# Experts in groups of 32 slots on four 32-column tiles of the array, results added back in quarter rows

## The chip, the cores and the metric

The kernel runs on one core of a Trainium2 chip. The metric is device time in microseconds of one execution. The engines of the core work side by side, each through its own program in order: TensorE (PE) multiplies and transposes, VectorE (DVE) and ScalarE (ACT) work element by element and empty PSUM, GpSimd (POOL) issues the indirect transfers and some element work, and SyncE (SP) issues nearly all other transfers. The 16 DMA engines of the core move what all queues ask for.

## The reference

One layer of a diffusion backbone over 512 latent tokens and 256 context tokens of width 1024, in 32-bit floats: modulated RMSNorm, one input projection, a gated short convolution beside grouped-query attention, an output projection with a gated residual, and then a mixture of experts, which takes most of the time:

```
logits = h @ w_router + b_router                 # 512 tokens x 32 experts
top_logit, top_idx = top_k(logits, 4); gate = softmax(top_logit)
for every expert e, over the tokens that chose it:
    gu = x @ w_gate_up[e] + b_gate_up[e]         # 1024 -> 2048
    y  = clamped_swiglu(gu) @ w_down[e] + b_down[e]   # 1024 -> 1024
    out[token] += gate * y
x = x + gt2 * out; return rmsnorm(x, g_final)
```

Each of the 32 experts has 8.39 MB of gate and up weights and 4.19 MB of down weights; they are read once. 2048 pairs of token and expert are spread over the experts. With the inputs used, the reference's router gives the largest expert 97 tokens, the next four 96, 94, 89 and 88, and the 17th by size 62.

## The kernel before

The first part (to about 330 us) computes norms, projections, attention, convolution and the router. Then the experts follow in an order of turns i = 0 to 31, sorted on chip by token count: `sort` ranks the experts, `place(i)` says which rank is worked on in turn i. Even turns are "heavy" (the 16 largest, 128 slots), odd turns are "light" (the other 16, 64 slots). What an expert has beyond its slots goes to a loop in `overflow`, which runs only if its block count is above zero. All engines meet at that branch, once.

Weights come in chunks of 1 MB, 128 partitions x 8 KB: 8 gate-up chunks `gu` (one for each 128 rows of the contraction) and 4 down chunks `dn` per turn. The list `seq` gives their order: of turn i first three gate-up chunks, then the four down chunks of turn i-1, then the other five gate-up chunks. `fetch` (L107 to L128) issues the next chunk of this list on SP's queue each time that a chunk has been used up; each fetch waits for PE to release the buffer that it refills, and for one of eight completion semaphores used in turn. There are 18 such buffers once all pools are open.

A heavy turn multiplies a chunk in four matmuls, 128 slots stationary and 512 weight columns moving, with the full array (L1017 gate-up, L1048 down). A light turn holds only 64 slots: two matmuls with 64 stationary columns each lie beside each other in the array, one for the low and one for the high half of the weight columns, so that slots 0 to 63 of PSUM hold one half of the output and partitions 64 to 127 the other (L1019, L1050). Each 32-bit matmul is two records in the trace. A bias matmul closes the gate-up sums (L1028, L1030).

Around them, per turn: `gather(i)` (L1200) reads the tokens' rows from the normed activations H2 by an indirect transfer on POOL's queue, `turn_x(i)` (L1212) transposes them, `activate` (L1224 to L1227) computes the clamped SwiGLU, `turn_a` (L1246) transposes its result, `put_back` weighs the down result by the gate (L1259, L1271) and `scatter` (L1253) adds it to ACC in HBM by an indirect accumulating transfer on POOL's queue. Each scatter waits for the one before it to land, since both add to ACC; POOL is in order, so what stands behind a waiting scatter waits too. Heavy and light turns have gather buffers of their own (`xgH`, `xgL`). The last turn's result is not scattered but multiplied back to the token rows on PE; ACC is read back (`sum` chunks) after the scatter of turn 30, added, normed and written out.

Of the kernel before, what the change touches and what calls it, by code (L numbers as in the profile page):

```python
# [35 lines left out]
P = 128  # L36
D = 1024
# [19 lines left out]
FULL = E // 2  # L57
CAP = 64
# [14 lines left out]
def dit_block(ctx, tc, x, c, cx, c_ctx, w_ada, b_ada, g_norm1, g_norm2, w_in, g_q, g_k, w_conv, w_out,  # L73
# [98 lines left out]
    nm2 = cst.tile([P, 1], F32)  # L172
# [86 lines left out]
    def place(i):  # L259

        return i // 2 if i % 2 == 0 else FULL + i // 2

# [36 lines left out]
    def places():  # L299
# [6 lines left out]
        half = float(SEQ + 1 + CAP)  # L306
# [4 lines left out]
        V.scalar_tensor_tensor(pm513, col[:, 0:1], -float(CAP), p513, op0=OP.mult, op1=OP.add)  # L311
        V.tensor_scalar(nm2, col[:, 0:1], -2.0, None, op0=OP.add)
        V.tensor_scalar(sgn, pm513, float(SEQ + 1 + E), -1.0, op0=OP.is_ge, op1=OP.mult)
# [639 lines left out]
    gt2l = m1.tile([P, 512], F32, name="gt2l")  # L953
    for _ in range(RING2):
        fetch()
    for q in range(4):
        DQ.dma_start(braw[q * E:(q + 1) * E, :].rearrange("e (m n) -> e m n", m=2),
                     raw_ap(b_gate_up, (q // 2) * 512, [[F2, E], [D, 2], [1, 512]]))
# [48 lines left out]

    def first_products(i, k):
        w, q = chunks.pop(("gu", i, k)), place(i)
        if k == 0:  # L1010
            gu[i] = [pair("S"), pair("R")] if heavy(i) else pair("J")
# [10 lines left out]
        if k < KC - 1:  # L1022
            return
        for m in range(2):
            b_ = bias[:, m * 512:(m + 1) * 512]
            if heavy(i):
                for n in range(2):
                    T.matmul(a[m][:, n, :], sel[:, n, q:q + 1].to_broadcast([P, P]), b_, start=False, stop=True)  # L1028
            else:
                T.matmul(a[:, m, :], sel2[i], b_, start=False, stop=True)  # L1030

    sel2 = {}

    def spread_sel(i):
        sel2[i] = m1.tile([P, 2 * CAP], F32R, name="sel2")
        V.tensor_copy(sel2[i].rearrange("p (n c) -> p n c", n=2),  # L1036
                      sel[:, :, place(i):place(i) + 1].to_broadcast([P, 2, CAP]))

    def second_products(i, j):
        w = chunks.pop(("dn", i, j))  # L1040
        if j == 0:
            dn[i] = pair("R") if heavy(i) else bank("V")
        for r in range(2):
            for n in range(2):
                c_ = slice(r * D + n * 512, r * D + (n + 1) * 512)
                start, stop = j == 0 and r == 0, j == 3 and r == 1
                if heavy(i):
                    T.matmul(dn[i][:, n, :], aT[i][:, 2 * j + r, :], w[:, c_], start=start, stop=stop)  # L1048
                else:
                    T.matmul(dn[i][n * CAP:(n + 1) * CAP, :], aT[i][:, j % 2 * 2 + r, j // 2 * CAP:(j // 2 + 1) * CAP],  # L1050
                             w[:, c_], start=start, stop=stop)
        fetch()

    sel = m1.tile([P, 2, E], F32R, name="sel")
    perm = m1.tile([2 * E, 2, E], F32, name="perm")
# [4 lines left out]
    at = cst.tile([2 * E, 1], F32)  # L1060

# [33 lines left out]

    tabs2 = cst.tile([P, 4, FULL], F32)
    idx = cst.tile([P, 2, FULL], I32)

    def slot_tables():

        p_ = bank("T")
        pv = perm.rearrange("p a e -> p (a e)")
        T.matmul(p_[:, 0:2 * E], tabA, pv, start=True, stop=True)
        for n in range(2):
            T.matmul(p_[n * CAP:(n + 1) * CAP, 2 * E:4 * E], tabA[:, 0:CAP], pv, start=True, stop=True)
        for h in range(2):
            V.tensor_copy(tabs2[:, h:4:2, :], p_[:, 2 * E * h:2 * E * h + 2 * E].rearrange(
                "p (a e) -> p a e", a=2)[:, :, FULL * h:FULL * h + FULL])
        ad_ = m1.tile([P, 2, FULL], F32, name="ad")
        V.tensor_scalar(ad_[:, 0, :], tabs2[:, 0, :], 0.0, p513, op0=OP.is_equal, op1=OP.mult)  # L1110
        V.tensor_scalar(ad_[:, 1, :], tabs2[:, 1, :], 0.0, pm513, op0=OP.is_equal, op1=OP.mult)
        V.scalar_tensor_tensor(idx[:, 0, :], tabs2[:, 0, :], -1.0, ad_[:, 0, :], op0=OP.add, op1=OP.add)
        V.tensor_add(ad_[:, 1, :], tabs2[:, 1, :], ad_[:, 1, :])
        V.tensor_scalar(idx[:, 1, :], ad_[:, 1, :], 2.0, nm2, op0=OP.mult, op1=OP.add)
        V.tensor_scalar(tabs2[:, 2:4, :], tabs2[:, 2:4, :], 1.0 / ALPHA, None, op0=OP.mult)

    def column(i):

        q = place(i) % FULL
        return idx[:, i % 2, q:q + 1], tabs2[:, 2 + i % 2, q:q + 1], tabs2[:, i % 2, q:q + 1]  # L1120


    def biases():
# [3 lines left out]
        V.tensor_scalar(braw[:, 512:D], braw[:, 512:D], 1.0, None, op0=OP.add)  # L1127
# [31 lines left out]
    def count_blocks(part):  # L1159

        if part == 0:
            nb = state["nb"] = m1.tile([E, NT + 2], F32, name="nb")
            V.tensor_scalar(nb[:, 0:1], at[0:E, :], float(FULL), float(P - CAP), op0=OP.is_ge, op1=OP.mult)
            V.tensor_add(nb[:, 0:1], nb[:, 0:1], cnt[0:E, :])
# [31 lines left out]
    H2h, ACCh = (x_.rearrange("r (n d) -> (r n) d", n=2) for x_ in (H2, ACC))  # L1196

    def gather(i):
        t = m2.tile([P, D if heavy(i) else 512], F32, name="xgH" if heavy(i) else "xgL")
        G.indirect_dma_start(out=t, out_offset=None, in_=H2[:, :] if heavy(i) else H2h,  # L1200
                             in_offset=bass.IndirectOffsetOnAxis(ap=column(i)[0], axis=0))
        xg[i] = t

    def turn_x(i):
        n = KC if heavy(i) else 4
        xT[i] = xp.tile([P, n, P], F32, name="xT", tag="xh" if heavy(i) else "xl")
        t = xg.pop(i)
        for hf in range(n // 4):
            p_ = bank("TV"[hf])
            for k in range(4):  # L1210
                kk = hf * 4 + k
                T.transpose(p_[:, k * P:(k + 1) * P], t[:, kk * P:(kk + 1) * P], ident)  # L1212
            if hf:
                V.tensor_copy(flat(xT[i][:, 4:8, :]), p_)
            else:
                S.activation(flat(xT[i][:, 0:4, :]), p_, AF.Copy)  # L1216
# [3 lines left out]
    def swiglu(pool, g, u, bufs=None):  # L1220

        more = {"bufs": bufs} if bufs else {}
        sg_ = pool.tile([P, 512], F32, name="sg", **more)
        S.activation(sg_, g, AF.Silu, scale=ALPHA)  # L1224
# [323 lines left out]
```

## Time and profile before

| | |
|---|---|
| three runs | 1482.43, 1475.53, 1480.48 us, median 1480.48 |
| the profiled execution | 1478.09 us, of which the trace's span is 1476.4 us |
| PE, PE weight load, DVE, ACT, POOL busy | 95%, 46%, 24%, 16%, 14% |
| traffic | 485 MB, mean 329 GB/s over the span |
| granted TensorE clock | 0.98 in the mean, 1.00 nearly everywhere between 384 us and 1440 us |

Busy is the share of time in which an engine had an instruction under way; a PE that is always busy is not a PE at its peak, since one matmul's record reaches past the start of the next. "DMA share" is the time that the packets took over the time of 16 engines; as packets overlap a little, it stands at 1.02 when the engines have work all the time.

### The profile page before, as it was taken

Reading aid. Unit: us, or ns where it says so; the run is one execution under the profiler, and the core shown is the slowest. Engines: PE = TensorE matmul, PEld = TensorE weight load, DVE = VectorE, ACT = ScalarE, POOL = GpSimd, SP = SyncE. Lnnn points to the kernel's source line nnn. Section 1 sums busy time; section 2 is a strip of 40 time slices with the busy share of each in tenths; the row PEclk is TensorE's granted clock in tenths of the full one; section 3 lists DMA queues with packets and bytes.
Section 4 is the critical chain, followed back from the end, with each engine's and each line's share of the span. In section 5 each row is a group of like instructions: output and inputs, shape, how many; then the busy total and the mean of one; then the engine's idle time right before and its main releaser. Section 6 shows DMA issues by size and latency. Waiting matters only on the chain.

```text
span 1476.4 us, 13652 instructions
## 1 busy us (share of the span) xinstructions
PE 1395.3 (95%) x5070; PEld 686.3 (46%) x5070; DVE 353.3 (24%) x655; ACT 230.1 (16%) x362; POOL 199.7 (14%) x152
## 2 busy tenths in 40 slices
PE   5899889997999999999999999999999999999994
PEld 1677668783344444444434444444444443434441
DVE  2796654554101010110110110101011011011014
ACT  1435555431000000000000000000000000000002
POOL 1412632203011000000010100000000000010011
PEclk9899999999999999999999999999999999999997
DMA  9446444157999999999999999999999999999922
GB/s 344 156 172 231 168 143 157 44 223 298 402 399 400 412 390 414 373 414 378 411 364 402 382 395 381 389 408 361 415 372 414 377 412 371 399 384 392 388 100 111
DMA packets 80831, 485.18 MB, mean 329 GB/s; under 512 B 9661, under 2 KB 9977, under 8 KB 28537
## 3 DMA queue, kind: packets, MB, share of 16 engines
q1 hardware_dynamic: 70978, 453.57, 77.0%
q0 software_dynamic: 9680, 30.68, 7.5%
q8 instruction: 41, 0.67, 0.2%
q14 instruction: 28, 0.23, 0.0%
q10 hardware_dynamic: 104, 0.03, 0.0%
HBM read 464.58 MB, written 19.66 MB: 328 GB/s over the span
## 4 chain that ended last, share of the span: by engine, by line
PE 73%; ACT 1%; DVE 0%; issue 0%; POOL 0%; POOLq 0%; ACTq 0%; DVEq 0%
PE J L1019 16%; PE R L1048 15%; PE S L1017 15%; PE R L1017 14%; PE V L1050 8%; PE S L1246 2%; PE T L1212 1%; PE J L1030 1%; ACT aH L1250 1%; PE T L1246 1%; PE S L1028 1%; PE R L1028 0%; PE V L1212 0%; DVE hl L1472 0%; POOL hl L1508 0%
## 5 line engine op out<-in xcount | busy, mean ns | idle before, releaser
L1017 PE MATMUL S<-raw,xT 128*128 128x512 f32 x348 | 166.5, 601 | 1.6 <-PEq L1281 1.6
L1017 PE MATMUL R<-raw,xT 128*128 128x512 f32 x348 | 163.5, 592 | 0.0
L1019 PE MATMUL J<-raw,xT 128*64 128x512 f32 x696 | 158.8, 598 | 0.0
L1048 PE MATMUL R<-raw,aH 128*128 128x512 f32 x320 | 140.8, 595 | 0.0
L1216 ACT ACTIVATE xT<-T 128x512 f32<-128x512 f32 x31 | 18.5, 597 | 712.5 <-PE T L1212 712.5
L1017 PEld LDWEIGHTS R<-raw,xT 128*128 128x128 f32 x348 | 66.2, 190 | 83.5 <-issue 83.5
L1253 POOL DMA_INDIRECT ACC<-y,idx x16 | 25.3, 1581 | 586.6 <-DVE sel L1036 586.6
L1017 PEld LDWEIGHTS S<-raw,xT 128*128 128x128 f32 x348 | 63.9, 192 | 73.3 <-issue 72.3
L1048 PEld LDWEIGHTS R<-raw,aH 128*128 128x128 f32 x320 | 60.0, 190 | 79.9 <-issue 79.9
L1226 DVE TENSOR_SCALAR lm<-R 128x512 f32<-128x512 f32 x32 | 22.1, 691 | 285.0 <-PE R L1028 284.4
L1019 PEld LDWEIGHTS J<-raw,xT 128*64 128x64 f32 x696 | 46.2, 136 | 90.0 <-issue 88.8
L1048 PE MATMUL R<-hl,aH 128*128 128x512 f32 x192 | 86.6, 605 | 0.0
L1050 PE MATMUL V<-raw,aL 128*64 128x512 f32 x352 | 80.7, 606 | 0.7 <-ACT aL L1250 0.7
L1259 DVE SCALAR_TENSOR_TENSOR y<-R,tabs,gt2r 128x512 f32<-128x512 f32 x32 | 22.5, 746 | 240.7 <-PE R L1048 240.7
L1017 PE MATMUL S<-hl,xT 128*128 128x512 f32 x164 | 77.6, 595 | 0.0
L1017 PE MATMUL R<-hl,xT 128*128 128x512 f32 x164 | 77.1, 592 | 0.0
L1253 POOL DMA_INDIRECT ACC<-yL,idx x15 | 24.5, 1632 | 378.2 <-DVE yL L1271 378.2
L1019 PE MATMUL J<-hl,xT 128*64 128x512 f32 x328 | 75.0, 599 | 0.0
L1271 DVE SCALAR_TENSOR_TENSOR yL<-V,tabs,gt2l 128x512 f32<-128x512 f32 x15 | 11.3, 751 | 236.3 <-PE V L1050 236.3
L1048 PEld LDWEIGHTS R<-hl,aH 128*128 128x128 f32 x192 | 36.5, 193 | 47.7 <-issue 47.7
L1017 PEld LDWEIGHTS R<-hl,xT 128*128 128x128 f32 x164 | 31.2, 190 | 39.2 <-issue 39.2
L1050 PEld LDWEIGHTS V<-raw,aL 128*64 128x64 f32 x352 | 24.5, 138 | 52.9 <-issue 52.0
(481 smaller groups left out, 1636.3 us busy)
## 6 DMA issues: line engine op xcount, KB each, us to landing
raw<-in_w_gate_up_dram SPq DMA_DIRECT2D x174, 1024.0 KB, 10.9
raw<-in_w_down_dram SPq DMA_DIRECT2D x84, 1024.0 KB, 12.9
hl<-in_w_gate_up_dram SPq DMA_DIRECT2D x82, 1024.0 KB, 10.3
hl<-in_w_down_dram SPq DMA_DIRECT2D x44, 1024.0 KB, 12.0
raw<-in_w_ada_dram SPq DMA_DIRECT2D x24, 1024.0 KB, 5.7
raw<-in_w_in_dram SPq DMA_DIRECT2D x10, 1024.0 KB, 8.3
raw<-in_w_out_dram SPq DMA_DIRECT2D x4, 1024.0 KB, 6.7
H<-t POOLq DMA_DIRECT2D x5, 512.0 KB, 2.9
```

Source lines behind the costliest of these rows:

```text
L1017: T.matmul(a[m][:, n, :], xT[i][:, k, :], w[:, c_], start=k == 0, stop=False)
L1019: T.matmul(a[n * CAP:(n + 1) * CAP, m, :], xT[i][:, k % 4, k // 4 * CAP:(k // 4 + 1) * CAP], w[:, c_], start=k == 0, stop=False)
L1028: T.matmul(a[m][:, n, :], sel[:, n, q:q + 1].to_broadcast([P, P]), b_, start=False, stop=True)
L1030: T.matmul(a[:, m, :], sel2[i], b_, start=False, stop=True)
L1048: T.matmul(dn[i][:, n, :], aT[i][:, 2 * j + r, :], w[:, c_], start=start, stop=stop)
L1050: T.matmul(dn[i][n * CAP:(n + 1) * CAP, :], aT[i][:, j % 2 * 2 + r, j // 2 * CAP:(j // 2 + 1) * CAP], w[:, c_], start=start, stop=stop)
L1212: T.transpose(p_[:, k * P:(k + 1) * P], t[:, kk * P:(kk + 1) * P], ident)
L1216: S.activation(flat(xT[i][:, 0:4, :]), p_, AF.Copy)
L1226: V.tensor_scalar(lm, u, LIMIT + 1.0, 1.0 - LIMIT, op0=OP.min, op1=OP.max)
L1246: T.transpose(p_[:, c_ * P:(c_ + 1) * P], r_[:, b0:b0 + 255:2], ident)
L1253: G.indirect_dma_start(out=to, out_offset=bass.IndirectOffsetOnAxis(ap=ix_, axis=0), in_=y, in_offset=None, compute_op=OP.add)
L1259: V.scalar_tensor_tensor(y[:, n * 512:(n + 1) * 512], a[n], g, gt2r[:, n * 512:(n + 1) * 512], op0=OP.mult, op1=OP.mult)
```

## The change

Three ranks of size take the place of two. The four largest experts have four groups of 32 slots (128), the next twelve three groups (96), the other sixteen two (64). The four-group experts are turns 0, 8, 16 and 24; the other even turns have three groups, the odd ones two. Every group is worked on alike in `strips`: its 32 slots are the stationary operand of four matmuls that lie side by side in the four 32-column tiles of the array, each with a different quarter of the weight columns. In gate-up a matmul moves 512 columns (256 gate and 256 up), in down 256. So the work on the array goes with the number of groups, and there are 4 matmuls per group and chunk in gate-up, 8 in down, where a chunk had 4 before in every turn.

The result of a group has a quarter of the model width in each 32 partitions, so ACC is seen as rows of 256 elements, and `put_back` issues one scatter of 128 such rows per group, where it issued one per expert. One gather buffer `xg` serves heavy and light turns, and every gather reads whole rows. The last turn keeps its 64-column down product. At the start of the expert part there are a few more small instructions: four ACT copies for `gt2q`, eight bias loads for four, and tables for four groups.

```diff
-FULL = E // 2
-CAP = 64
+STEPS = (4, 16)
+W = 32
+HALF = 64
...
+    def groups(i):
+        return 4 - sum(place(i) >= s for s in STEPS)
...
+    for j in range(4):
+        S.activation(gt2q[W * j:W * j + W, :], gt2[W * j:W * j + W, j * 256:(j + 1) * 256], AF.Copy)
...
+    def strips(i, o, lhs, w, start, stop, per=1):
+        n = groups(i)
+        for g in range(n):
+            for j in range(4):
+                T.matmul(o(g)[j * W:(j + 1) * W], lhs(g), w(j), start=start and g % per == 0,
+                         stop=stop and (g % per == per - 1 or g == n - 1), skip_group_check=per > 1)
     def first_products(i, k):
-        for m in range(2):
-            for n in range(2):
-                c_ = slice(m * D + n * 512, m * D + (n + 1) * 512)
-                if heavy(i):
-                    T.matmul(a[m][:, n, :], xT[i][:, k, :], w[:, c_], start=k == 0, stop=False)
-                else:
-                    T.matmul(a[n * CAP:(n + 1) * CAP, m, :], xT[i][:, k % 4, k // 4 * CAP:(k // 4 + 1) * CAP], w[:, c_],
-                             start=k == 0, stop=False)
+        strips(i, lambda g: a[g // 2][:, g % 2, :], lambda g: xT[i][:, k, g * W:(g + 1) * W], lambda j: w[:, j],
+               k == 0, False)
         fetch()
...
     def second_products(i, j):
...
+                strips(i, lambda g: quarter(dn[i], g), lambda g: aT[i][:, g, r, j * W:(j + 1) * W],
+                       lambda n: w[:, r * D + n * 256:r * D + (n + 1) * 256], start, stop, 2)
...
     def slot_tables():
-        T.matmul(p_[:, 0:2 * E], tabA, pv, start=True, stop=True)
+        for g in range(4):
+            for j in range(4):
+                T.matmul(p_[j * W:(j + 1) * W, 2 * E * g:2 * E * g + 2 * E], tabA[:, g * W:(g + 1) * W], pv,
+                         start=True, stop=True)
...
     def gather(i):
-        t = m2.tile([P, D if heavy(i) else 512], F32, name="xgH" if heavy(i) else "xgL")
-        G.indirect_dma_start(out=t, out_offset=None, in_=H2[:, :] if heavy(i) else H2h,
-                             in_offset=bass.IndirectOffsetOnAxis(ap=column(i)[0], axis=0))
+        n = groups(i) * W
+        t = m2.tile([n, D], F32, name="xg")
+        G.indirect_dma_start(out=t, out_offset=None, in_=H2[:, :],
+                             in_offset=bass.IndirectOffsetOnAxis(ap=idx[0:n, q:q + 1], axis=0))
...
     def put_back(i):
-        if heavy(i):
-            y = m1.tile([P, D], F32, name="y", bufs=2)
-            weigh(y, (a[:, 0, :], a[:, 1, :]), g)
-            scatter(y, ix_)
-        else:
-            y = m2.tile([P, 512], F32, name="yL")
-            V.scalar_tensor_tensor(y, a, g, gt2l, op0=OP.mult, op1=OP.mult)
-            scatter(y, ix_, ACCh)
+        for g in range(groups(i)):
+            V.scalar_tensor_tensor(y[:, g, :], quarter(a, g), gates4[:, g, q:q + 1], gt2q, op0=OP.mult, op1=OP.mult)
+        for g in range(groups(i)):
+            scatter(y[:, g, :], idx4[:, g, q:q + 1], ACCq)
```

TensorE's program at the end of a heavy turn's gate-up product and the start of the light one behind it, one row for each wait or run of like matmuls. S, R and J are PSUM banks, `raw` and `hl` weight buffers, `xT` the transposed tokens, `aH` the transposed SwiGLU result, `sg` that result itself; the shape is stationary columns x moving columns. Before:

```order
L1017 MATMUL S<-raw,xT 128x512
L1017 MATMUL R<-raw,xT 128x512 x2
L1028 MATMUL S<-bias,sel 128x512 x2
L1028 MATMUL R<-bias,sel 128x512 x2
L1019 MATMUL J<-raw,xT 64x512 [waits DMAHW0_49,Activation_49]
L1019 MATMUL J<-raw,xT 64x512 x3
```

And the same place after (a heavy turn of three groups):

```order
L1024 MATMUL S<-raw,xT 32x512 [waits DMAHW3_49]
L1024 MATMUL S<-raw,xT 32x512 x7
L1024 MATMUL R<-raw,xT 32x512 x4
L1038 MATMUL S<-bias,selx 128x512 [waits DVE_49]
L1038 MATMUL S<-bias,selx 128x512 x3
L1038 MATMUL R<-bias,selx 128x512 x2
L1024 MATMUL J<-raw,xT 32x512 [waits DMAHW4_49,Activation_49]
L1024 MATMUL J<-raw,xT 32x512 x7
```

A chunk of the heavy turn is 12 matmuls of 32 columns for four of 128, a chunk of the light one 8 of 32 for four of 64, and the bias takes six matmuls for four.

POOL's program from the scatter of one turn to the next two. ACC is the sum in HBM, `y` and `yL` the weighed results of heavy and light turns, `xgH`, `xgL` and `xg` the gathered tokens; DMASW semaphores belong to POOL's own transfers. Before:

```order
L1253 DMA ACC<-yL,idx 1280x512 [waits DMASW1_49,DVE_49]
L1200 DMA xgH<-H_807,idx 128x1024 [waits DMASW0_49,PE_49]
L1253 DMA ACC<-y,idx 640x1024 [waits DMASW3_49,DVE_49]
L1200 DMA xgL<-H_807,idx 128x512 [waits DMASW2_49,PE_49]
L1253 DMA ACC<-yL,idx 1280x512 [waits DMASW5_49,DVE_49]
```

After:

```order
L1289 DMA ACC<-yL,idx_2435 2560x256 [waits DMASW2_49,DVE_49]
L1289 DMA ACC<-yL,idx_2435 2560x256 [waits DMASW4_49,DVE_49]
L1225 DMA xg<-H_809,idx 96x1024 [waits DMASW3_49,PE_49]
L1289 DMA ACC<-y,idx_2435 2560x256 [waits DMASW5_49,DVE_49]
L1289 DMA ACC<-y,idx_2435 2560x256 [waits DMASW7_49,DVE_49]
L1289 DMA ACC<-y,idx_2435 2560x256 [waits DMASW0_49,DVE_49]
L1225 DMA xg<-H_809,idx 64x1024 [waits DMASW6_49,PE_49]
```

Three scatters of 128 quarter rows stand where one of 128 whole rows stood, and two where one of half rows stood; each waits for the one before, and the next gather stands behind the last.

## Rows read from the trace of the kernel before

**Rows 1.** Windows: us, busy us of each engine, clock, DMA share, GB/s.
```profile
352.00:1408.00 1056.00, 1042.07 (x3394) 437.04 (x3393) 122.66 (x200) 63.22 (x108) 86.67 (x72) 1.00 1.00 393
1408.00:1440.30 32.30, 31.61 (x113) 12.42 (x111) 5.00 (x8) 1.68 (x3) 4.98 (x9) 1.00 0.19 52
1440.30:1476.40 36.10, 14.85 (x60) 5.29 (x58) 15.51 (x39) 10.48 (x23) 7.00 (x3) 0.75 0.28 106
```
**Rows 2.** SP's queue, waits: who it waited for, us in total, times, longest.
```profile
SPq L127 <- PE R L1017: 378.0, 123, 4.1
```
**Rows 3.** Chain that ended last, in order of time: start us, us, engine, line, records.
```profile
1210.63 13.93 PE R L1048 x32
1224.57 7.02 PE J L1019 x32
1245.92 7.02 PE V L1050 x32
```
**Rows 4.** Timeline of POOL, 1185 to 1255 us.
```profile
1185.42 1.58 POOL L1253 DMA_INDIRECT ACC<-yL,idx  x1 [24.83 <-DVE yL L1271]
1226.29 1.58 POOL L1253 DMA_INDIRECT ACC<-y,idx  x1 [38.00 <-DVE sel L1036]
1254.01 1.58 POOL L1253 DMA_INDIRECT ACC<-yL,idx  x1 [24.84 <-DVE yL L1271]
```
**Rows 5.** Windows of 3 us in that pair, and the pair itself.
```profile
1189.00:1192.00 3.00, 3.00 (x8) 1.33 (x7) 0.00 (x0) 0.00 (x0) 0.00 (x0) 1.00 1.03 365
1231.00:1234.00 3.00, 3.00 (x20) 1.34 (x16) 0.69 (x1) 0.60 (x1) 0.00 (x0) 1.00 1.00 318
1246.00:1249.00 3.00, 3.00 (x16) 1.00 (x16) 0.00 (x0) 0.00 (x0) 0.00 (x0) 1.00 1.02 423
1185.42:1254.01 68.59, 67.90 (x223) 28.41 (x223) 7.83 (x12) 4.07 (x7) 5.14 (x4) 1.00 0.99 389
```
**Rows 6.** Timeline of PE in the first part: matmuls of 32 and of 64 columns.
```profile
27.17 1.07 PE L376 MATMUL S<-raw,c 128*32 128x512 f32 x8 [1.90 <-DMA raw<-in_w_ada_dram]
30.09 1.94 PE L381 MATMUL J<-raw,c 128*64 128x512 f32 x8 [1.86 <-DMA raw<-in_w_ada_dram]
```
**Rows 7.** DMA queues of the page: packets, MB, share of 16 engines.
```profile
q1 hardware_dynamic: 70978, 453.57, 77.0%
q0 software_dynamic: 9680, 30.68, 7.5%
```
**Rows 8.** DMA issues: count, KB each, median us from issue to landing.
```profile
hl<-ACC SPq DMA_DIRECT2D x4, 512.0 KB, 5.9
xgL<-H,idx POOLq DMA_INDIRECT x16, 11.9
ACC<-y,idx POOLq DMA_INDIRECT x16, 11.7
ACC<-yL,idx POOLq DMA_INDIRECT x15, 9.0
```
**Rows 9.** Timeline at the end, 1426 to 1458 us.
```profile
1432.05 1.56 POOL L1253 DMA_INDIRECT ACC<-y,idx  x1 [39.29 <-DVE sel L1036]
1438.23 1.75 SPq L127 DMA_DIRECT2D hl<-ACC  x4
1440.26 0.74 PE L1030 MATMUL J<-bias,sel 128*128 128x512 f32 x2
1456.34 1.28 DVE L1472 TENSOR_TENSOR hl<-hl,S 128x512 f32<-128x512 f32 x2
```
**Rows 10.** Timeline where the expert part begins: ACT's copies, PE at the branch.
```profile
324.45 1.25 ACT L979 ACTIVATE gt2l<-acc 64x512 f32<-64x512 f32 x2
360.86 1.95 PE L1017 MATMUL S<-raw,xT 128*128 128x512 f32 x4 [1.61 <-PEq L1281]
```
**Rows 11.** Windows of 4 us, granted clock in the third column from the right.
```profile
376.00:380.00 4.00, 1.61 (x9) 1.40 (x10) 2.73 (x5) 1.06 (x2) 0.00 (x0) 0.96 1.01 424
380.00:384.00 4.00, 4.00 (x7) 1.69 (x6) 0.53 (x1) 0.00 (x0) 0.00 (x0) 0.61 1.01 424
```

More of the change, by code (lines that the diff above doesn't have):

```diff
@@ L953, in dit_block @@
     gt2l = m1.tile([P, 512], F32, name="gt2l")
+    gt2q = m1.tile([P, 256], F32, name="gt2q")
     for _ in range(RING2):
@@ L1043, in second_products, with quarter @@
         for r in range(2):
[L1044 to L1051, printed above, removed]
+            start, stop = j == 0 and r == 0, j == 3 and r == 1
+            if i == E - 1:
+                for n in range(2):
+                    T.matmul(dn[i][n * HALF:(n + 1) * HALF, :], aT[i][:, r * 4 + j, :],
+                             w[:, r * D + n * 512:r * D + (n + 1) * 512], start=start, stop=stop)
+            else:
+                strips(i, lambda g: quarter(dn[i], g), lambda g: aT[i][:, g, r, j * W:(j + 1) * W],
+                       lambda n: w[:, r * D + n * 256:r * D + (n + 1) * 256], start, stop, 2)
         fetch()
+    def quarter(o, g):
+        return (o[:, g // 2, :] if len(o.shape) == 3 else o)[:, g % 2 * 256:g % 2 * 256 + 256]
     sel = m1.tile([P, 2, E], F32R, name="sel")
+    selx = m1.tile([P, 4, HALF], F32R, name="selx")
     perm = m1.tile([2 * E, 2, E], F32, name="perm")
@@ new lines, in slot_tables @@
+        T.matmul(p_[:, 256:256 + E], tabA, perm[:, 0, :], start=True, stop=True)
+        for n in range(2):
+            T.matmul(p_[n * HALF:(n + 1) * HALF, 320:384], tabA[:, 0:HALF], pv, start=True, stop=True)
+        v = p_[:, 0:256].rearrange("p (g a e) -> p g a e", g=4, a=2)
+        tmp = t4.tile([P, 2, 4, E], F32, name="t4")
+        toks4, ad_ = tmp[:, 0], tmp[:, 1]
+        V.tensor_copy(toks4, v[:, :, 0, :])
+        V.tensor_scalar(gates4, v[:, :, 1, :], 1.0 / ALPHA, None, op0=OP.mult)
@@ new lines, in slot_tables @@
+        V.tensor_copy(last2, p_[:, 320 + E - 1:384:E])
+        V.tensor_scalar(gate_last, last2[:, 1:2], 1.0 / ALPHA, None, op0=OP.mult)
+        row = m1.tile([P, E], F32, name="row")
+        V.tensor_copy(row, p_[:, 256:256 + E])
+        V.tensor_scalar(ad_[:, 0, :], row, 0.0, p513, op0=OP.is_equal, op1=OP.mult)
+        V.scalar_tensor_tensor(idx, row, -1.0, ad_[:, 0, :], op0=OP.add, op1=OP.add)
+        V.tensor_scalar(ad_, toks4, 0.0, pm513, op0=OP.is_equal, op1=OP.mult)
+        V.tensor_add(ad_, toks4, ad_)
@@ L1123, in biases @@
+        V.tensor_scalar(idx4, ad_, 4.0, nm4, op0=OP.mult, op1=OP.add)
     def biases():
@@ L1230, in activate @@
     def activate(i):
-        a = gu.pop(i)
-        if heavy(i):
-            act[i] = [swiglu(m2, a[0][:, n, :], a[1][:, n, :], 3) for n in range(2)]
-        else:
-            act[i] = [swiglu(m2, a[:, 0, :], a[:, 1, :], 3)]
+        a, n = gu.pop(i), groups(i)
+        act[i] = [(swiglu(m2, o[:, 0:min(2, n - 2 * q), 0:256], o[:, 0:min(2, n - 2 * q), 256:512], 3),
+                   min(2, n - 2 * q)) for q, o in enumerate(a)]
     def turn_a(i):
@@ L1262, in put_back @@
     def put_back(i):
-        ix_, g, _ = column(i)
-        a = dn.pop(i)
-        if heavy(i):
-            y = m1.tile([P, D], F32, name="y", bufs=2)
-            weigh(y, (a[:, 0, :], a[:, 1, :]), g)
-            scatter(y, ix_)
-        else:
-            y = m2.tile([P, 512], F32, name="yL")
-            V.scalar_tensor_tensor(y, a, g, gt2l, op0=OP.mult, op1=OP.mult)
-            scatter(y, ix_, ACCh)
+        q, a = place(i), dn.pop(i)
+        y = (m1 if heavy(i) else m2).tile([P, groups(i), 256], F32, name="y" if heavy(i) else "yL",
+                                          **({"bufs": 2} if heavy(i) else {}))
+        for g in range(groups(i)):
+            V.scalar_tensor_tensor(y[:, g, :], quarter(a, g), gates4[:, g, q:q + 1], gt2q, op0=OP.mult, op1=OP.mult)
+        for g in range(groups(i)):
+            scatter(y[:, g, :], idx4[:, g, q:q + 1], ACCq)
         del xT[i], aT[i]
@@ L1398, in rows_back @@
         for t in range(NT):
-            G.tensor_scalar(fin[:, t:t + 1], column(LAST)[2], -1.0 - P * t, None, op0=OP.add)
+            G.tensor_scalar(fin[:, t:t + 1], last2[:, 0:1], -1.0 - P * t, None, op0=OP.add)
             G.tensor_scalar(b_[:, t, :], iota, fin[:, t:t + 1], None, op0=OP.is_equal)
@@ L1429, in dit_block @@
             gather(2)
-        if kind == "gu" and k == LEAD and not heavy(i):
+        if kind == "gu" and k == LEAD and i > 0:
             spread_sel(i)
```

147 lines of the change are left out of this document (78 added, 69 removed).

## The prediction

> **What bounds the kernel now.** I read the busy shares by window first, then SP's waits, then the chain that ended last, then one pair of turns, heavy and light, in the timeline. [...] SP waits for PE to release weight buffers, 378.0 us for L1017 alone [rows 2]. So PE is the bound. [...] That PE is behind, and not the transfers, is seen at the end: from 1408 us on the share is 0.19, and PE still multiplies landed weights until 1440.26 [rows 1, 9].
>
> The scatter of a light turn comes again after 68.59 us (1185.42, then 1254.01 [rows 4, 5]), the time of a pair. In it PE is busy 67.90 us [rows 5]. A heavy chunk costs 13.93 / 4 = 3.48 us, a light one 7.02 / 4 = 1.755 [rows 3]; twelve of each are 41.8 + 21.1 = 62.9, and 5.7 us are left for transposes, bias and gaps. The transfers of a pair would need 68.59 x 0.99 / 1.02 = 66.6 us if they never paused [rows 5]. So whatever PE is given, a pair can't fall under about 66.6 unless the bytes or the packets change.
>
> **The change, part by part.**
>
> *Products.* 32-column matmuls do run side by side four at a time: in the first part eight records (four matmuls) take 1.07 us, where eight of 64 columns, two at a time, take 1.94 [rows 6]. If four tiles keep the rate that two have in a long run, a group costs half a light chunk, 0.878 us: 2.63 for three groups, 1.755 for two as before, 3.51 for four. A pair of three and two groups is 60 group-chunks = 52.7 us, one of four and two 72 = 63.2. I put the rest at 8 us instead of 5.7: four more transposes for a light turn, ten bias matmuls for six (0.74 us for two at the end of a sum [rows 9]), more switches between tiles and the whole array. That makes 60.7 and 71.2 us, and 63.3 in the mean of four pairs (one has a four-group turn). The trace doesn't show a long run of 32-column matmuls, nor their 256-column form, in which four times as many matmuls come in a microsecond as in a light turn's down product. From below 0.878 bounds it; from above the lone burst, 1.07 with its filling and draining each time. I take 0.878, since the burst holds one end of the array's pipeline which a run shares out.
>
> *What is late next.* 63.3 is under 66.6, so the transfers become the bound. The eighteen buffers cover the four-group pair (71.2), whose excess of 5 us the next pairs win back at 6 us each.
>
> *Transfers.* Weights are the same. Gathers and scatters of a pair fall from 1.57 MB to 1.31 (five groups for six of 128 KB, both ways). The software queue, which holds them, took 7.5% of 1476 us for 30.68 MB, 3.6 us per MB [rows 7]: by bytes a pair gains 1.0 us. Against it stand five scatters of 128 rows of 1 KB for two of 4 and 2 KB. A row of any length could cost the same: if half of the 5.7 us that 1.57 MB take are scatters, five for two would add 4.3 us to a pair. Between these ends the landing times are the nearest rows: a scatter of twice the bytes lands 2.7 us later (11.7 against 9.0 [rows 8]), so the cost goes mostly with bytes, and a small scatter would land in 9.0 - 1.35 = 7.7 us. I take no change, between -1.0 and +4.3.
>
> *The queue of scatters.* Each waits for the last. A turn of three needs 23 us, four 31, two 15; POOL is in order, so the gather two turns ahead goes out behind them and lands 11.9 us later [rows 8]. It is needed one turn (33 us) and four chunks (10 us) after the scatters begin, 43 us: 23 + 12 = 35 fits, 31 + 12 = 43 just does. I cost it at nothing; where it is late, at four turns, the weight buffers hide it.
>
> *Setup.* Four ACT copies of 32 partitions more (two of 64 took 1.25 us [rows 10]), and some ten small DVE instructions before the branch, where PE already idles 1.61 us [rows 10]. SP fetches behind both: 3 us, between 0 and 6. The four further bias loads lie beside an idle stretch of the queue: nothing.
>
> *The sum.* Against the profiled execution (span 1476.4, own time 1478.09; the median of the runs is 1480.48, 2.4 above it). The weights now end at about 1409. The share falls short of 1.02 by 0.02 over 1056 us, 21 us; 20 of them go, 3 come at the start: 1392. The last gate-up chunk lands four down chunks ahead, 10 us at 1.05 MB and 423 GB/s, and PE, which follows now, is done with it 2 us later: 1384, where it was 1440.26 [rows 9]. From there it was 36.1 us to the end [rows 1]: 1420. Two additions: the last scattered turn has three groups, its down product ends near 1375, its chain of 23 us near 1399, and the four reads of ACC land 5.9 us later [rows 8], 1405, with the first add due at 1384 + 16 = 1400 [rows 9] and the others over some 4 us: 2 us. PE's lag behind the last chunk: 2 us. The span is 1424, the execution 1426; beside the median I say **1428 us**.
>
> *The clock.* With the transfers as bound PE waits for chunks in light turns, 1.755 busy in some 2.6. [...]
>
> [...] In the first part four tiles give 1.94 / 1.07 = 1.8 times what two give [rows 6]. [...]
>
> **The rivals.** One number parts three cases, the time p of a group's chunk; the mean pair has 63 of them and 8 us. Up to p = (66.6 - 8) / 63 = 0.93 the transfers bind. Up to (68.59 - 8) / 63 = 0.96 PE binds and is still faster.
>
> 1. PE stays the bound and is only a little faster: tile switches and the short 256-column matmuls cost some 6% more, p = 0.94, pair 67.2. 1.4 us x 15.5 pairs = 22 us: 1458. For it: nobody has shown the run of small matmuls; against it: in light turns 64-column matmuls keep 7.02 us for 32 records without loss [rows 3].
>
> 2. Slower: PE can't feed four tiles. Each group pays the burst's 1.07 us, because the instructions, twice as many per group in down, or the weight loads, don't come fast enough. Mean pair 63 x 1.07 + 8 = 75.4, 6.8 us more, 15.5 times: 1585; halfway, at p = 1.0, 71 us and 1518. It decides from p = 0.96. For it: the stretch to 0.96 is 9%; against it: in the burst eight records, their loads included, fit in 1.07 us.
>
> 3. Scatters are dear. At +4.3 us per pair the transfers need 70.9: the weights end 67 us later and the whole near 1495; at a third of it 1450. For it: 1 KB rows occur nowhere in the expert part, and in the 3 us after a heavy scatter the traffic is 318 GB/s, after a light one 365, against 423 [rows 5]; against it: that very difference goes with the bytes.
>
> That the change does not do what it says could come from an expert with more tokens than slots, which would run the overflow loop. The counts of these inputs (97, then 96 to 88, the 17th 62) fit 128, 96 and 64.
>
> **How the numbers follow.** A run of this kernel tells a difference of about 0.5% (7 us) from none: same is 1473 to 1488. The forecast has 0.58, and its own range is 1410 to 1445 (scatters by bytes, 16 us, and all pauses gone below; setup, clock and lag above). Rival 1 has 0.16, 1445 to 1472. Rival 2 has 0.14, rival 3 has 0.12, half of it under 1473, the rest split between same and slower. Faster: 0.58 + 0.15 + 0.05 = 0.78; same: 0.01 + 0.02 + 0.03 = 0.06; slower: 0.16, with 0.01 for late gathers. The range for 8 in 10 takes in the forecast and rival 1: 1408 to 1475.
>
> **What would show it.** Right: over the expert stretch the DMA share is 1.02 nearly throughout and PE's idle time is ended by weight transfers, not by other engines; SP waits less for PE and more for earlier transfers; three-group chunks follow each other at 2.63 us; the last weights land near 1392 and the last gate-up product ends some 8 us before. Wrong: SP still waits for PE and groups take over 0.96 us (rival 2); the share is full but the weights end near 1410 or later (rival 3); POOL's gathers end PE's idle time, or the reads of ACC hold up the first add by more than 5 us.

## The result and the profile after

The changed kernel takes 1439.29 us (median of four runs, 1437.77 to 1441.29) where the kernel before takes 1480.28 on the same chip (1475.53 to 1482.43): a ratio of 0.9728, 95% interval 0.9700 to 0.9756. The forecast said 1428 us in a range of 1408 to 1475, faster with a chance of 0.78. The direction and the bound that it named are right; it is 11 us too low. The profiled execution has a span of 1436.1 us, where the forecast's sum ended at 1424.

Windows of the changed kernel, in the columns of [rows 1]: the expert stretch, and six windows of 4 us near its end.

```profile
384.00:1340.00 956.00, 905.78 (x10320) 375.28 (x10319) 109.36 (x224) 58.09 (x103) 153.89 (x116) 0.99 1.03 396
...
1384.00:1388.00 4.00, 4.00 (x80) 2.41 (x76) 0.00 (x0) 0.00 (x0) 0.00 (x0) 1.00 1.01 418
1388.00:1392.00 4.00, 4.00 (x50) 1.84 (x40) 1.40 (x4) 0.00 (x0) 1.54 (x1) 1.00 1.00 413
1392.00:1396.00 4.00, 4.00 (x38) 1.20 (x40) 0.00 (x0) 0.00 (x0) 0.00 (x0) 1.00 0.80 296
1396.00:1400.00 4.00, 4.00 (x35) 1.38 (x28) 0.00 (x0) 0.00 (x0) 0.00 (x0) 1.00 0.56 213
1400.00:1404.00 4.00, 1.24 (x7) 0.63 (x5) 1.38 (x2) 0.98 (x2) 1.54 (x1) 1.00 0.64 229
1404.00:1408.00 4.00, 3.96 (x10) 1.07 (x10) 0.42 (x1) 0.00 (x0) 0.00 (x0) 0.57 0.46 153
```

The DMA share is 1.03 throughout, where [rows 1] had 1.00; PE is busy 95% of the stretch instead of 99%. The long stretch of landed weights that PE still had to multiply, 32.3 us at a share of 0.19 in [rows 1], is gone. New is the end: from about 1393 us on the share sinks to half while weights are still landing, up to 1406.8. Nothing in the forecast speaks of that.

SP's waits, to be read against the 378.0 us for PE's release of buffers in [rows 2]:

```profile
SPq L128 <- DMA raw<-in_w_gate_up_dram: 308.4, 138, 4.3
SPq L128 <- DMA hl<-in_w_gate_up_dram: 161.2, 72, 4.4
SPq L128 <- DMA raw<-in_w_down_dram: 159.3, 70, 4.3
SPq L128 <- PE R L1024: 83.7, 44, 10.2
```

SP waits for its own earlier transfers now, and PE waits for weights. Three pieces of the chain that ended last, in the columns of [rows 3], show both the pace of the groups and the new wait:

```profile
717.72 10.36 PE R L1024 x192
728.08 6.87 PE J L1024 x64
...
764.97 23.31 DMA raw<-in_w_gate_up_dram
```

The first is the down product of a three-group turn, twelve group-chunks in 10.36 us, 0.863 each; the second is four gate-up chunks of a light turn, 1.72 each. The light chunk of [rows 3] was 1.755. The third is the time of one weight chunk from issue to landing. POOL's timeline of one four-group and one light turn, as in [rows 4], and the landings, as in [rows 8]:

```profile
1193.59 1.55 POOL L1289 DMA_INDIRECT ACC<-y,idx  x1 [26.57 <-DVE y L1303]
1202.63 1.54 POOL L1289 DMA_INDIRECT ACC<-y,idx  x1 [7.49 <-DMA ACC<-y,idx]
1212.58 1.54 POOL L1289 DMA_INDIRECT ACC<-y,idx  x1 [8.41 <-DMA ACC<-y,idx]
1222.65 1.54 POOL L1289 DMA_INDIRECT ACC<-y,idx  x1 [8.53 <-DMA ACC<-y,idx]
1224.50 0.94 POOL L1225 DMA_INDIRECT xg<-H,idx  x1 [0.30 <-PE R L1024]
```

```profile
ACC<-y,idx POOLq DMA_INDIRECT x52, 9.1
xg<-H,idx POOLq DMA_INDIRECT x31, 10.5
ACC<-yL,idx POOLq DMA_INDIRECT x30, 8.9
```

A scatter of 128 rows of 1 KB lands after 9 us, as late as the one of 2 KB before. The queues, as in [rows 7], with a third that matters below:

```profile
q1 hardware_dynamic: 71298, 453.58, 79.2%
q0 software_dynamic: 16640, 27.53, 8.1%
q8 instruction: 102, 1.67, 0.5%
```

The software queue takes more time for fewer bytes, and the instruction queue brings 102 packets of 16 KB where the kernel before had 41.

From the packet records between 420 and 1370 us one can count what a pair costs each of the sixteen engines (sum of the packets' times over 16, per 3072 weight packets of 8 KB). The pair itself is measured between the landings of chunks 60 and 396, counted over all transfers with rows of 8 KB, of which 24 come ahead of the experts:

```
us per pair          before  changed  half rows  full    full, light as before, step 2
weights               62.1    61.9     61.0      60.3    60.3
gathers                1.9     2.2      2.0       2.0     2.0
scatters               4.0     4.4      4.4       4.4     4.0
instruction fetches   0.11    0.36     0.35      0.34    0.27
pair, measured        68.46   67.55    66.35     65.76   65.59
```

The three columns on the right are experiments, told next.

### The profile page after: what moved, and what is told of

Same layout as the page of the kernel before. It is cut to its first block, busy times and chain, and to the rows that moved or that the text cites. A ratio compares the mean times of both kernels' runs of the same rounds, so it can differ in the third digit from the quotient of the medians.

```text
span 1436.1 us, 29286 instructions
## 1 busy us (share of the span) xinstructions
PE 1308.5 (91%) x12798; PEld 642.9 (45%) x12798; DVE 350.1 (24%) x715; ACT 229.1 (16%) x366; POOL 274.9 (19%) x203
## 4 chain that ended last, share of the span: by engine, by line
DMA 39%; PE 32%; issue 1%; DVE 1%; ACT 1%; POOL 0%; ACTq 0%; SPq 0%; POOLq 0%; DVEq 0%
DMA raw<-in_w_gate_up_dram 18%; PE R L1024 11%; PE J L1024 7%; PE S L1024 7%; DMA raw<-in_w_down_dram 6%; DMA hl<-in_w_gate_up_dram 5%; DMA ACC<-y,idx 5%; DMA hl<-in_w_down_dram 3%; DMA xg<-H,idx 3%; PE V L1024 2%; PE S L1275 1%; PE T L1239 1%; PE S L1038 1%; PE V L1049 1%; PE J L1038 1%
## 5 line engine op out<-in xcount | busy, mean ns | idle before, releaser
L1289 POOL DMA_INDIRECT ACC<-y,idx x52 | 80.6, 1550 | 575.5 <-DVE y L1303 279.0
L1024 PE MATMUL S<-raw,xT 128*32 128x512 f32 x1392 | 174.1, 616 | 4.6 <-DMA raw<-in_w_gate_up_dram 2.7
L1024 PE MATMUL J<-raw,xT 128*32 128x512 f32 x1392 | 159.3, 595 | 5.0 <-DMA raw<-in_w_gate_up_dram 4.9
L1024 PE MATMUL R<-raw,aH 128*32 128x256 f32 x2048 | 113.9, 379 | 1.3 <-DMA raw<-in_w_down_dram 1.2
L1024 PE MATMUL R<-raw,xT 128*32 128x512 f32 x880 | 113.6, 604 | 0.0
L1024 PEld LDWEIGHTS R<-raw,aH 128*32 128x32 f32 x2048 | 66.3, 110 | 50.4 <-issue 6.0
L1024 PE MATMUL V<-raw,aL 128*32 128x256 f32 x1280 | 74.5, 385 | 8.6 <-DMA raw<-in_w_down_dram 8.6
L1024 PE MATMUL S<-hl,xT 128*32 128x512 f32 x656 | 80.4, 606 | 0.6 <-DMA hl<-in_w_gate_up_dram 0.6
L1024 PE MATMUL J<-hl,xT 128*32 128x512 f32 x656 | 75.6, 595 | 5.1 <-DMA hl<-in_w_gate_up_dram 5.0
L1024 PE MATMUL R<-hl,aH 128*32 128x256 f32 x1280 | 72.3, 383 | 0.0
```

The costliest lines, as they stand in the source:

```text
L1024: T.matmul(o(g)[j * W:(j + 1) * W], lhs(g), w(j), start=start and g % per == 0, stop=stop and (g % per == per - 1 or g == n - 1), skip_gro ...
L1289: G.indirect_dma_start(out=to, out_offset=bass.IndirectOffsetOnAxis(ap=ix_, axis=0), in_=y, in_offset=None, compute_op=OP.add)
```

## The experiments

The changed kernel was run again beside the first three. As expected: 

> The changed kernel once more, as the measure for the three runs beside it: 1439 us as before (1437 to 1441), the landings of a weight transfer on the sixteen DMA engines 15 us apart late in the expert stretch, the last weights at 1407 us of the span.

It took 1438.59 us (1436.99 to 1443.22); late in the stretch the sixteen landings of one weight transfer lie 14 to 17 us apart, and the last weights land at 1408.9. All differences below are against it where nothing else is said.

**Gathers of light turns into 128 partitions.** The edit, cut to its core (`idxh` is a table of half-row numbers, as in the kernel before):

```diff
-        t = m2.tile([n, D], F32, name="xg")
-        G.indirect_dma_start(out=t, ..., in_=H2[:, :], in_offset=...(ap=idx[0:n, q:q + 1], axis=0))
+        t = m2.tile([P, 512], F32, name="xgL", tag="xg")
+        G.indirect_dma_start(out=t, ..., in_=H2h, in_offset=...(ap=idxh[:, ...], axis=0))
```

> One part is undone: a light turn's 64 rows are gathered as 128 half rows of 2 KB, as in the kernel before, and turned in four transposes; all else as changed. Theory A (the gather of 64 rows of 4 KB uses eight of the sixteen DMA engines, so that in every pair these eight fall behind the others; at the end the others stand idle while the eight finish): the landings of a weight transfer stay 2 to 5 us apart instead of growing to 15, no half-used stretch at the end, last weights 6 us earlier from the missing lag and some 3 to 5 us earlier because full gathers cost less (128 packets of 2 KB at 80 ns for 64 at 207 ns: 0.2 us a pair), time 1428 to 1432. Theory B (the lag comes from the 96-row gathers or from the scatters): the spread grows as in the changed kernel and the time stays within 4 us of 1439. Theory C (the engines' lag is real but costs nothing): the spread goes and the time stays within 2 us of 1439.

Measured: 1423.97 us (1419.36 to 1424.61), ratio to the kernel before 0.9609 (0.9595 to 0.9624), 14.6 us faster than the changed kernel. None of the three theories has it right: the time fell by more than theory A says, and yet the landings of a weight transfer come to lie 15 us apart as before, so A's cause is wrong; how many engines a gather uses no record shows. What fell is the pair, 67.60 to 66.35, and the table shows where: in the weight packets. Windows of 3 us that hold a 64-row gather, first in the changed kernel, then in this run, with GB/s last:

```profile
756.90:759.90 3.00, 3.00 (x32) 0.91 (x28) 0.00 (x0) 0.00 (x0) 0.00 (x0) 1.00 1.02 319
815.20:818.20 3.00, 3.00 (x32) 0.78 (x24) 0.00 (x0) 0.00 (x0) 1.11 (x1) 1.00 1.03 314
```

```profile
819.00:822.00 3.00, 3.00 (x36) 0.91 (x32) 0.00 (x0) 0.00 (x0) 0.69 (x1) 1.00 1.04 433
1016.30:1019.30 3.00, 3.00 (x36) 0.91 (x28) 0.00 (x0) 0.00 (x0) 0.76 (x1) 1.00 1.01 424
```

The share is full in both, but a quarter of the traffic is missing where the rows go into 64 partitions. In the trace the gather is 64 packets of 4 KB in either run, so it is the place that they go to that differs. There a gathered packet of 4 KB takes 212 ns and the weight packets beside it 423 ns in the mean; into 128 partitions they take 159 to 163 and 309. So the traffic is 314 to 319 GB/s with 64 partitions against 424 to 433 with 128, and the next windows show that gathers into 96 are nearly as slow, at 335 to 336. What makes the packets slow there no trace here shows.

**Heavy gathers into 128 partitions too.** On top of the run before, a heavy turn gathers all 128 slots, also where it multiplies 96.

```diff
         n = groups(i) * W
...
+        n = P
         t = m2.tile([n, D], F32, name="xg")
```

> Light turns gather 128 half rows, as in the run before, and heavy turns gather all 128 slots, also where only 96 of them are multiplied; all else as changed. Theory A (a gather into 64 or 96 partitions is dear beside weights: the 96-row one has packets of 200 ns instead of 159 and slows the weight packets beside it from 309 to 395 ns, 1.2 + 0.7 us of every engine; one into 128 partitions takes 1.27 and slows nothing; and the uneven load makes eight engines lag): against 1424 of the run with half rows alone the pair loses 0.6 us, 15 pairs 9 us, the landings of a weight transfer stay 2 to 3 us apart, and the half-used stretch at the end goes, 6 us: 1407 to 1413. Theory B (the slow packets come from the gathers, but the lag from the scatters): 9 us from the packets, the spread still grows: 1414 to 1417. Theory C (32 rows more cost their bytes): 1424 + 15 x 0.3 = 1428 or more.

Measured: 1414.52 us (1411.65 to 1415.01), 0.9555 (0.9537 to 0.9573): more bytes and 9.4 us less, as A and B say and C doesn't. The landings still move apart, to 14 to 16 us as before, and the time is theory B's; B's reason for the lag, the scatters, is tested by the next run. Windows of 4 us with a 96-row gather in the changed kernel, and with a 128-row gather here:

```profile
900.40:904.40 4.00, 4.00 (x33) 1.50 (x35) 2.77 (x4) 1.19 (x2) 0.00 (x0) 1.00 1.03 336
982.30:986.30 4.00, 4.00 (x82) 2.41 (x76) 0.00 (x0) 0.00 (x0) 0.00 (x0) 1.00 1.04 335
```

```profile
900.10:904.10 4.00, 4.00 (x33) 1.51 (x36) 2.77 (x4) 1.19 (x2) 0.00 (x0) 1.00 1.02 423
981.80:985.80 4.00, 4.00 (x80) 2.45 (x76) 0.00 (x0) 0.00 (x0) 0.00 (x0) 1.00 1.03 424
```

The changed kernel has a control of its own: its few gathers of 128 rows have packets of 160 ns, with weight packets of 311 ns beside them, where those of 96 rows have 201 and 398. Together the two edits are worth 24 us: that is the price of gathering into 64 and 96 partitions. Why 96 are nearly as dear as 64 is open.

**Fewer and longer scatters.** Two groups go out as one scatter of 2 KB rows, to wrong rows.

```diff
-        for g in range(groups(i)):
-            scatter(y[:, g, :], idx4[:, g, q:q + 1], ACCq)
+        for g in range(0, groups(i), 2):
+            n = min(2, groups(i) - g)
+            scatter(y[:, g:g + n, :]..., idx[:, q:q + 1] if n == 2 else idx4[:, g, q:q + 1], ACCh if n == 2 else ACCq)
```

> The scatters of two groups go out as one scatter of 128 rows of 2 KB, to rows that are not theirs; the same bytes in 48 scatters instead of 82, and the output means nothing. Theory A (an accumulating packet costs 101 ns for 1 KB and 176 ns for 2 KB, so short rows cost transfer time): 34 x 128 x (202 - 176) / 16 = 7 us of every engine's time, weights end 7 us sooner, 1431 to 1434. Theory B (the packets' extra time lies in gaps that others fill): within 2 us of 1439. Theory C (POOL's chain of scatters holds up the gathers and with them PE): more than 12 us, below 1427, and the waits of PE's transposes for the gathered rows (21 us in 5 waits) go.

Measured: 1438.21 us (1434.00 to 1442.05), the same time: theory B. The packets' times do fall by 0.55 us a pair, but so does the DMA share, 1.027 to 1.021, and the pair by 0.2 alone: many short packets overlap more. Theory C falls too. In the changed kernel PE waits for late gathers (its waits: us in total, times, longest),

```profile
PE T L1239 <- DMA xg<-H,idx: 21.0, 5, 6.1
```

and in this run that wait is not there, without a gain. The landings lie 15 us apart as before, so neither the number nor the length of the scatters sets the lag.

**Less PE work where transfers bind.** The turns of rank 2 and 3 get three groups: `STEPS = (2, 16)`.

> The turns of rank 2 and 3 get three groups instead of four (rank 0 and 1 keep four); all else as changed. Theory A (the transfers bind, in the pairs with four groups too): PE does 2 x 12 group-chunks less, 24 x 0.86 = 21 us, none of which shows; a scatter less (0.8 us) stands against a gather into 96 partitions for one into 128 (0.6 us): 1437 to 1440. Theory B (PE binds in the pairs with four groups and the weight buffers don't carry them): 1439 less 8 to 20 us.

Measured: 1440.54 us (1438.77 to 1442.27). PE's busy time falls by 21 us, 905.78 to 884.84 between 384 and 1340, and none of it shows; theory B is out.

```profile
384.00:1340.00 956.00, 884.84 (x10048) 369.90 (x10052) 105.16 (x223) 57.91 (x104) 150.11 (x114) 0.99 1.03 395
```

A first try of this kind went one rank further, `STEPS = (1, 16)`.

> The three turns of rank 1 to 3 get three groups instead of four (rank 0 alone keeps four); all else as changed. Theory A (the transfers bind, also in the pairs with four groups): PE does 3 x 12 group-chunks less, 36 x 0.86 = 31 us, and none of it shows; 3 x 32 rows less to gather and 3 x 128 packets of 1 KB less to scatter give 3 us: 1435 to 1438. Theory B (PE binds in the pairs with four groups and the weight buffers don't carry them): 1439 less 10 to 25 us, 1414 to 1429.

Measured: 1615.59 us (1612.79 to 1619.29), and it says nothing on the two theories: an expert beyond rank 0 has more than 96 tokens on the chip (the reference's router gives the second and third 96 and 94), so the overflow loop ran for one block of 128 slots. POOL issues the weight loads of that block 10.6 to 12.9 us apart, each behind PE's product of the one before, and the window of them shows a DMA share of 0.29:

```profile
345.00:540.00 195.00, 103.74 (x269) 42.07 (x269) 36.30 (x131) 4.64 (x7) 13.16 (x17) 0.68 0.29 100
```

**All heavy turns with four groups.** `STEPS = (16, 16)`: the tiles and the quarter rows without the slots that they save.

> All sixteen heavy turns keep four groups, 128 slots as in the kernel before; the four-tile matmuls, the quarter rows and all else as changed. Theory A (four tiles at once keep the rate of two, 0.86 us a group, and the gain is in the slots that are left out): 72 group-chunks x 0.863 = 62.1 and 8 us beside them make PE's pair 70 us, over the 67.7 us of the transfers: PE binds again, SP waits for PE, and the time is 1480 + 15 x 1.6 = 1504, 1494 to 1515, slower than before. Theory B (the tiles or the quarter rows bring the gain): 1455 or less.

Measured: 1519.57 us (two runs, 1515.29 and 1523.84), ratio 1.0271 (1.0232 to 1.0310): slower than the kernel before, as theory A says, though by 15 us more than it forecast, since the pair takes 71.10 us and not 70. SP waits for PE again:

```profile
SPq L128 <- PE R L1024: 588.5, 184, 9.9
SPq L128 <- PE J L1024: 217.6, 120, 3.5
```

**PE's own pace.** Half of each weight row is fetched, and all products are made from it. The edit's core, without the columns that the matmuls read:

```diff
+        if key[0] in ("gu", "dn") and 2 <= key[1]:
+            to, ap = to[:, :, 0:1024], ap[:, :, 0:1024]
         DQ.dma_start(to, ap)
```

> From the third expert on a transfer brings 4 KB of a row of weights instead of 8 KB, and the matmuls read what there is twice: all of PE's work on half of the bytes, so the output means nothing. Theory A (PE's own mean pair is about 62.4 us, 63 x 0.863 + 8, and the transfers' 67.6 set the pace): the pair falls to 61 to 64 us, the time to 1439 - 15 x 5 = 1365, 1345 to 1385, with a DMA share near 0.6. Theory B (PE is close behind the transfers, 66 us or more): 1415 or more.

Measured: 1378.02 us in one run; theory A. Between SP's issues of weight chunks that lie eight pairs apart 495.5 us pass, 61.9 a pair (eight, since every fourth pair has a four-group turn), with PE busy 99% and a DMA share of 0.75:

```profile
400.00:1320.00 920.00, 909.62 (x10491) 382.32 (x10484) 110.25 (x230) 60.18 (x107) 157.76 (x120) 1.00 0.75 228
```

**Fewer instructions for PE.** The trace has sixteen landing records for each weight chunk, and the page counts sixteen DMA engines. I take each landing for one engine's part; no record names its engine. Read so, the landings show how far apart the engines are. In the run with full gathers, two instruction fetches and the landings of one weight chunk before and after each (us after its first; worked out from the trace's landing records, sorted):

```
532.4: 0.0 0.0 0.5 0.5 0.6 0.6 1.1 1.2 1.7 1.8 2.0 2.1 2.1 2.2 2.3 3.4
       a fetch of 16 KB at 534.7, 1.04 us
537.3: 0.0 0.0 0.5 0.5 0.6 0.6 1.1 1.2 1.7 1.8 2.0 2.1 2.2 2.3 3.4 3.7
       a fetch of 16 KB at 541.4, 1.01 us
552.9: 0.0 0.0 0.5 0.5 0.6 0.6 1.1 1.6 1.7 1.9 2.1 2.2 2.3 3.5 3.7 4.0
```

After each fetch one more landing stands at 3.4 us or later. Between 375 and 1125 us the later eight landings move away from the earlier eight by 10.6 us in the changed kernel, with 64 fetches; the eighth and the ninth landing then lie 5 us apart. To test it, groups after the first were left out of the six middle gate-up chunks of each turn and of its two middle down chunks; the transfers stay.

```diff
-        for g in range(n):
+        for g in range(1 if thin else n):
```

> Of the six middle gate-up chunks of a turn and the two middle down chunks only the first group is multiplied; every transfer stays, the output means nothing. PE's instructions fall from 1444 to some 970 a pair. Theory A (every 256 PE instructions cost one instruction fetch of 16 KB, which holds one of eight DMA engines for 1 us, and that is why eight of the sixteen fall behind): fetches from 420 to 1370 us 80 -> 54, the landings of a weight transfer late in the stretch 10 us apart instead of 15, pair 0.1 us shorter, half-used stretch at the end 9 us instead of 13, time 1434 to 1437. Theory B (the scatters or the gathers make them lag): 15 us apart as before, time within 2 us of 1439.

Measured: 1432.70 us (1430.12 to 1432.90), 5.9 us faster (0.9677 of the kernel before, 0.9664 to 0.9690, where the changed kernel beside the other runs had 0.9721, 0.9705 to 0.9737): theory A, and 1 us beyond its range. Most of it comes where A doesn't say: the pair falls from 67.60 to 67.23, which is 5 us in fourteen pairs and not 0.1 a pair, and the last twelve chunks take 36.8 us for 38.9. An estimate from the packets gives most of it: fetches fall from 0.36 to 0.22 us a pair spread over sixteen engines, so eight engines, if they carry them all, are freed of 0.28. PE's lighter work by itself is an unlikely cause: in the run with three groups at rank 2 and 3 PE works 21 us less, with 77 fetches for 80, and nothing is gained. Its fetches over the whole run, and those of the mixed kernel that follows, against 102:

```profile
q8 instruction: 69, 1.13, 0.3%
```

```profile
q8 instruction: 82, 1.34, 0.4%
```

Between 420 and 1370 us the records have 20316 matmuls and weight loads with 80 fetches in the changed kernel, 12655 with 49 here, 16164 with 64 in the mixed one and 6161 with 24 before: one fetch for 253 to 258 instructions each time. The lag of the later eight landings over 375 to 1125 us goes with them: 10.6 us for 64 fetches, 6.0 for 41, 9.0 for 51, 0.15 to 0.18 a fetch. As an estimate, a fetch of 1.02 us on one of eight engines makes 0.13; what makes the rest is open. The kernel before had 20 fetches in that time and a lag of 0.3 only: there PE was the bound, and my explanation is that what was behind could catch up while SP waited for buffers [rows 2]. The run with four groups in all heavy turns is the test of that: it has 67 fetches in the same time, more than the changed kernel, but PE is its bound, and the lag doesn't grow (between the means of the later and the earlier eight landings 0.75 us at 375, 0.66 at 1125). So in these runs the fetches go with a lag where the transfers are the bound, and with next to none where PE is.

**A version from these findings.** The kernel with full gathers, whose light turns go back to 64-column tiles, two at a time, with one scatter of half rows:

```diff
-        strips(i, lambda g: a[g // 2][:, g % 2, :], ...)
+        if heavy(i): strips(...)
+        else: T.matmul(a[n * HALF:(n + 1) * HALF, m, :], xT[i][:, k % 4, k // 4 * HALF:(k // 4 + 1) * HALF], w[:, ...], ...)
```

> The kernel with full gathers (1414.5 us), in which light turns are as in the kernel before: 64-column tiles two at a time, one scatter of half rows (2 KB); heavy turns stay in groups. Theory A (the transfers bind; short rows and fetches are priced by their packets): a light turn's scatter costs 128 x 176 / 16 = 1.41 us instead of 256 x 101 / 16 = 1.62, PE's instructions fall by some 320 a pair (1.25 fetches, 0.08 us), 15 x 0.3 = 4 us, and the lag of eight engines falls from 14 to 11 us, 1.5 us at the end: 1407 to 1411, PE's 64-column chunks as fast as two groups (1.755 against 1.73). Theory B (light turns in groups gain PE time that counts): 1414 or more.

Measured: 1410.42 us (1407.98 to 1415.21), 0.9536 (0.9519 to 0.9553), 4.1 us under the run with full gathers, in A's range, though the intervals of the two ratios overlap. The number is A's, but not by A's sum: the pair is 65.71 for 65.76, 0.7 us in all where A had 4, the last twelve chunks are 1.7 us shorter (A had 1.5), and 3.0 of the 5.4 us by which the last weights land sooner were there by chunk 60. That last part I can't assign: chunk 60 lands at 422.7 here, at 425.7 with full gathers and at 426.1 in the next run, which begins alike. With `STEPS = (2, 16)` on top:

> The run beside it, and the turns of rank 2 and 3 get three groups instead of four. Theory A (the transfers bind still): two scatters less, 1.6 us, and PE's 21 us don't show: 1405 to 1409. Theory B (at 65.5 us a pair PE's four-group pairs, 70 us, have become too long for the buffers): 1395 to 1404.

Measured: 1408.06 us (1405.41 to 1414.23), ratio 0.9519 (0.9498 to 0.9540), in A's range; the two can't be told apart. It is the fastest here, 72 us under the kernel before and 31 under the changed one.

## Why the prediction was right, and where it was off

*Products.* The forecast took 0.878 us for a group's chunk, as the bound from below, and 63.3 us for PE's mean pair; measured are 0.863, a little under that bound, and 61.9. What the change wins lies in the slots that it leaves out: with four groups in every heavy turn it is 40 us slower than the kernel before. Rivals 1 and 2, which asked for 0.94 and more, are out.

*What is late next.* The transfers, as forecast; a share of 1.03, SP's waits and the two runs with less PE work, whose time follows the transfers, show it.

*Transfers.* This is the step that failed. It counted gathers by bytes ("by bytes a pair gains 1.0 us") and took the pair as unchanged at 66.6 us; measured are 67.55. The gathers lost bytes and became dearer, since their rows no longer reach all 128 partitions: 24 us by the two runs that undo it. With that undone the pair is 65.76, so the rest of the step was too high by 0.8; it started from weight packets of 323 ns in the kernel before, and with full gathers they take 314. Nearly all of that difference lies in a few long packets: 737 of 42713 took over 500 ns before, and 156 of 44423 with full gathers. With four groups in all heavy turns, where PE binds too, there are 1161, and in the changed kernel 491 of 43228. So these runs have more of them where PE binds and the queue pauses; what makes them is open.

*Scatters.* Nearly unchanged in cost, as said: their packets take 4.4 us a pair instead of 4.0. Rival 3 is out, since 34 scatters fewer gave nothing. The landing of 7.7 us was too low, 9.1. That a chain of four still takes the 31 us of the forecast is luck: it counted four landings, but the gather goes out right behind the issue of the fourth scatter, after three waits of 9.0 to 10.1 us. PE waits 21.0 us in all for gathers; the weight buffers hide it, as said.

*Setup.* 3.0 us at chunk 60 (422.4 for 419.4), as forecast. Its parts are another matter, so that the number is luck: the next weight chunk behind the eight bias loads on SP's queue is issued at 329.12, where it was 321.99, and the step had put these loads at nothing.

*The sum.* The last weights landed at 1410.4 before. From there 3.0 for the start, 14 x 0.91 = 12.7 less for the pairs and 6.0 more for the last twelve chunks, which take 38.7 us instead of 32.7 in the half-used windows shown first, make 1406.7; measured are 1406.8, forecast 1392. The missing 15 us are thus 7 of the pair, 6 of the lag of the later eight landings, which no term had, and 1 in reading the end. The forecast's sum itself had gone by the share, 20 us, which is 1.4 us a pair and not the 1.9 that 66.6 would give; with 66.6 it would have missed by more. By the signs that it set, 1406.8 lies nearer to rival 3's 1410 than to its own 1392; only the run with fewer scatters tells the two apart. The last gate-up product ended 7.5 us before the last weights (said: 8), and the rest took 36.8 us (said: 40), with the reads of ACC holding up the first add by 0.9. Those 3 us too many in the forecast hide part of the 15. The timeline of PE, SP and DVE at the end, as in [rows 9]:

```profile
1399.30 1.21 PE L1038 MATMUL J<-bias,selx 128*128 128x512 f32 x4
...
1412.76 1.76 SPq L128 DMA_DIRECT2D hl<-ACC  x4
...
1416.25 1.28 DVE L1508 TENSOR_TENSOR hl<-hl,S 128x512 f32<-128x512 f32 x2 [0.42 <-DMA hl<-ACC]
```

The add comes 16.95 us after the last gate-up product's bias, where it was 16.1.

*Clock.* The sum has no time for it, and the range counts some above. No run shows time lost to it: the granted clock is 0.99 over the stretch. With a third of PE's work left out it fell to 0.87 between 384 and 1340 us, and the time still fell:

```profile
384.00:1340.00 956.00, 695.05 (x6572) 267.90 (x6568) 107.53 (x223) 58.71 (x104) 156.08 (x118) 0.87 1.03 397
```

## What to carry over

When a change moves the bound from an engine to the transfers, price every small transfer by what it does to the large ones beside it: into how many partitions it goes counted more here than its bytes, 24 us for gathers into 64 and 96 partitions, though filling the 96 up to 128 brings more bytes. What cost nothing while an engine was the bound, such as instruction fetches or landings that drift apart (a lag of 0.3 us before, 10.6 in the changed kernel), is then paid, here in the pace of each pair and again at the end. And gather a few rows too many rather than fill part of the partitions: 32 rows more in the turns of three groups made the run 9.4 us shorter.

## What the runs showed of the hardware

A gather into 64 or 96 partitions beside saturated transfers took the traffic from 422 to 433 GB/s down to 314 to 336, at a DMA share that stays over 1; its packets took 201 to 212 ns and the weight packets 398 to 423 in the mean, instead of 159 and 309.

Every 253 to 258 matmuls and weight loads of PE went with a fetch of 16 KB, one packet of 1.0 us (80 fetches for 20316 instructions, 49 for 12655). With transfers as the bound, the later eight of the sixteen landings of a weight chunk fell behind the earlier eight by 0.15 to 0.18 us a fetch, until the first and last lay 15 us apart; with PE as the bound the lag did not grow over 67 fetches (0.75 us at 375, 0.66 at 1125).

An accumulating packet took 101 ns for 1 KB, 176 for 2 KB and 327 for 4 KB, against 159 for a gathered 4 KB; yet 7 us of such packet time saved in all gave no time, with the DMA share at 1.021 instead of 1.027: the short packets had overlapped more.

Four 32-column tiles kept in a long run what two 64-column tiles have, 0.863 us a group and chunk against 1.755 for two.
